# One wide matmul for the high and low rows in the up projection of a gated ConvFFN block

## The chip, the cores and the metric

The kernel runs on one core of a Trainium2 chip. The metric is the device time of one execution in microseconds. The engines are PE (TensorE: matmuls, and PEld for its weight loads), DVE (VectorE), ACT (ScalarE), POOL (GpSimd) and SP (SyncE, which here only issues transfers). Each works through its own queue in order; semaphores between them tell when a result is there.

## The reference

A decoder block with 512 rows and 2048 channels: a recurrent mixer and a windowed attention side by side, then a feed-forward part. All is float32. The change concerns the first product of the feed-forward part:

```python
D_MODEL = 2048
SEQ = 512
D_FF = 5632

def conv_ffn(h, w_up, conv_w, conv_b, w_down):
    u = h @ w_up                                   # (512, 2048) @ (2048, 11264)
    S = u.shape[1]
    up = jnp.pad(u, ((0, 0), (CONV_W - 1, 0), (0, 0)))
    c = up[:, 0:S] * conv_w[0] + up[:, 1:S + 1] * conv_w[1] + up[:, 2:S + 2] * conv_w[2] + conv_b
    val, gate = jnp.split(c, 2, axis=-1)
    return (jax.nn.silu(gate) * val) @ w_down
...
        x = x + conv_ffn(rms_norm(x, norm2_g[l]), w_up[l], conv_w[l], conv_b[l], w_down[l])
```

## The kernel before

The kernel runs in stages: the input projections with mixer and attention, the branch and out products, the **up products** of the feed-forward part with its convolution and gate, and the down products.

*Precision.* A float32 product is made of three faster ones. A weight tile is split into a high part `whi` (rounded by ACT, L1105) and the rest `wlo` (DVE, L1107), and the rows into `xh` and `xl` likewise. The sum is `whi*xh + whi*xl + wlo*xh`: three matmuls, each with its own weight load, into the same PSUM columns (L1122 to L1125).

*Blocks and products.* The up projection works on 44 blocks `f`. A block has 128 value columns and 128 gate columns of the weights; with the two halves of the contraction that is a 2 x 2 of weight tiles (`a11`, `a12`, `a22` and sums), against a 2 x 2 of the rows (two halves of 256 rows, `TH`, and two halves of the contraction, each of `KH` = 8 pieces of 128). A scheme with seven products in place of eight gives the four quarters of the result `u`: P1, P2, P5, P6, P7, Q4 and P3. Each product is 8 x 3 matmuls of 256 columns. The rows' factors lie in SBUF for the whole stage as pairs of tiles `bq[name] = [high, low]` (`b11`, `b21`, `b22`, `t1` to `t4`).

*PSUM.* A block uses three tiles, each a full bank of 512 columns, of which a steady block uses the first 256. X takes P1, P6, P5 and P3 one upon the other and is read after each of them; P7 and Q4 share Y; P2 has Z. A `start` flag is set on the first matmul of P1, P7 and P2.

*What follows a product* (`Block.out`, L1127 to L1156): after P1, P6, P5 and P3 ACT copies X to a quarter of `u` (L1152); after P2, P5 and Q4 DVE adds Z or Y to a quarter (L1154, L1156). `Block.conv` (L1161 to L1185) makes the convolution in five or seven pieces: ACT scales (L1173) and makes the SiLU (L1179), DVE multiplies and adds (L1176, L1181); in odd blocks `factors` (L884 to L888) then forms four factors for the down products, and `Block.keep` (L1187) issues three DMAs for them on ACT's queue (L893 to L895).

*The order* is written out by hand. `steps` lists (block, product); in a steady block it is P7, P6, P2, P5, then P1 of the next block, Q4, P3. `run(i)` first calls `prep(i + 2)`: the weight sum of P6 and P3 (DVE, L1100), one waiting piece of a convolution, `whi` (ACT) and `wlo` (DVE) for the step after next, and the loads that have become possible; then it issues the matmuls of step i, then `out`. There are three buffers for `whi` and `wlo`, and ACT and DVE run at most two products ahead of PE. Every such instruction is wrapped in `pin`, which keeps the written order on its engine.

*Loads.* SP issues 512 KB weight loads (L1091) as buffers come free; POOL adds a second load onto one in flight for the sums s3 and s1 (L1093), and makes sums of down weights on the side (L239).

The blocks 0 to 6 have a special order of their own, and so has block 43.

Of the kernel before, what the change touches and what calls it, by code (L numbers as in the profile page):

```python
# [8 lines left out]
F32 = mybir.dt.float32  # L9
F32R = mybir.dt.float32r  # L10
# [3 lines left out]
ALU = mybir.AluOpType  # L14
# [4 lines left out]
P = 128  # L19
S = 512  # L20
# [114 lines left out]
def block_kernel(ctx: ExitStack, tc: tile.TileContext, d: Dims, a: dict, out: bass.AP):  # L135
    nc = tc.nc
    act, dve, pool, pe, sync = nc.scalar, nc.vector, nc.gpsimd, nc.tensor, nc.sync
    NK, NP, NQ, NKV, NF = d.NK, d.NP, d.NQ, d.NKV, d.NF
# [16 lines left out]
    NPRE = 4  # L155
# [50 lines left out]
    pin = tc.keep_in_program_order  # L206
# [13 lines left out]
    for f in range(NPRE):  # L220
        w, t = a["w_up"][f], {n: up_d[f, n] for n in ("s3", "s1", "P6", "P3")}
# [70 lines left out]
    if True:  # L292
# [3 lines left out]
        with tc.tile_pool(name="x0_ps", bufs=6, space=PSUM) as ps0:  # L296
# [10 lines left out]
            for h in range(2):  # L307
                hs = slice(h * HT * P, (h + 1) * HT * P)
                for k in range(NK):
                    ps = ps0.tile([P, HT * P], F32, name="ps_x", tag="x")  # L310
# [45 lines left out]
        with ExitStack() as pt:  # L356
# [4 lines left out]
            def small():  # L361
                return mps.tile([P, S], F32, name="mi", tag="mi")
# [26 lines left out]
            for t in range(NKV):  # L389
# [12 lines left out]
                ps = small().rearrange("p (n c) -> p n c", c=P)  # L402
                for b in range(NT):
                    pe.transpose(ps[:, b], vf[:, b * P : (b + 1) * P], ident)
                ps = ps.rearrange("p n (h c) -> p n h c", c=HD)
# [14 lines left out]
            for g in range(NHK):  # L420
# [7 lines left out]
                for n in range(NT):  # L428
# [32 lines left out]
                    for kb in kbs:  # L461
                        ps = small().rearrange("p (h c) -> p h c", c=P)
# [3 lines left out]
                    ps = small()  # L466
                    for kb in kbs:
                        for i in range(2):
                            pe.matmul(ps, vhl[:, n - 1 + kb, g].rearrange("p e c -> p (e c)"),
                                      phl[i][:, kb].rearrange("p h c -> p (h c)"),  # L470
                                      start=kb == kbs[0] and i == 0, stop=kb == kbs[-1] and i == 1)
                    ol = ap_.tile([HD, S], F32, name="ol", tag="ol", bufs=2)
                    act.activation(ol, ps[HD:P], AF.Copy)
                    ps, ol = (x[0:HD].rearrange("p (e j c) -> p e j c", e=2, c=P) for x in (ps, ol))
# [6 lines left out]
        with ExitStack() as pr:  # L481
# [8 lines left out]
            for i in range(2):  # L490
                z = zp_.tile([P, S + 1], F32, name=f"zpad{i}")
# [8 lines left out]
            def wtile(tag, bufs=1):  # L500
                return wk.tile([P, S], F32, name=tag, tag=tag, bufs=bufs)
# [20 lines left out]
            for i in range(NG):  # L522
                acc = ztile(d.c_gd + i * P)
                t = wtile("lw")
# [347 lines left out]
    KH = NK // 2  # L872
    TH = S // 2
# [26 lines left out]
    with ExitStack() as pbb:  # L900
# [8 lines left out]
        for m, i in order:  # L909
            hi, lo, r0, n, gi = parts[i]  # L910
# [11 lines left out]
            if second:  # L922
                w = min(XC, d.D)
                for e in range(m * XC, (m + 1) * XC, w):
                    t, c0 = divmod(e, d.D)
# [81 lines left out]

    upx = ExitStack()
    bqp = upx.enter_context(tc.tile_pool(name="bqA", bufs=1, reuse_waits="tile"))
    bq = {n: [bqp.tile([P, KH, TH], F32R, name=f"{n}{i}") for i in range(2)] for n in ("b11", "b21")}  # L1010
    hp = hps.enter_context(tc.tile_pool(name="hhlO", bufs=3, reuse_waits="tile"))
    NCC = d.D // S
    ssp = tcp.tile([P, NT, NCC], F32, name="ssp")
# [62 lines left out]
    us = []  # L1076
    dve.tensor_scalar(cw[:, 0:3, NF:], cw[:, 0:3, NF:], -1.0, None, op0=ALU.mult)

    class Block:

        def __init__(self, f):
            self.f, self.w, self.hl = f, {}, {}
            self.apart = 2 <= f < NPRE

        def load(self, n):
            f, w = self.f, self.w
            at = {"a11": (0, 0), "a12": (0, 1), "s3": (0, 0), "s1": (1, 0), "a22": (1, 1)}
            w[n] = raw_tile("a11", 2) if own(f, n) else raw_tile()  # L1090
            sync.dma_start(w[n], up_d[f, n] if (f, n) in up_d else a["w_up"][(f, *at[n])])  # L1091
            if n in ("s3", "s1") and f >= NPRE:
                pool.dma_start(w[n], a["w_up"][f, 1, int(n == "s1")], accum_op=ALU.add)  # L1093
# [15 lines left out]
        def mm(self, n):  # L1109
            if n == "P1":  # L1110
                x = ups.tile([P, S], F32, name="X", tag="X")
                self.X = x[:, :TH]
                self.Z = x[:, TH:] if self.f < NPRE else upy.tile([P, S], F32, name="Z", tag="Y")[:, :TH]
            if n == "P7":
                self.Y = upy.tile([P, S], F32, name="Y", tag="Y")[:, :TH]
            into = {"P2": "Z", "P7": "Y", "Q4": "Y"}.get(n, "X")
            ps = getattr(self, "Z" if self.apart and n in ("P5", "P3") else into)
            start = n in ("P1", "P7") or n == "P2" and self.f >= NPRE or n == "P5" and self.apart
            whi, wlo = (x.rearrange("p (k c) -> p k c", c=P) for x in self.hl.pop(n))
            xh, xl = bq[{"P1": "b11", "P2": "b21", "P7": "t3", "P6": "t2", "P5": "t1", "Q4": "t4", "P3": "b22"}[n]]  # L1120
            for k in range(KH):
                last = k == KH - 1  # L1122
                for i, (l, r) in enumerate(((whi, xh), (whi, xl), (wlo, xh))):
                    pin(pe.matmul(ps, l[:, k], r[:, k], start=start and k + i == 0, stop=last and i == 2,  # L1124
                                  skip_group_check=True))  # L1125

        def out(self, n):  # L1127
            if n == "P7":
                return
            X, Y, Z = self.X, getattr(self, "Y", None), self.Z  # L1130
            if n == "P1" and self.f < NPRE:
                self.t1 = up.tile([P, TH], F32, name="t1", tag="t1", bufs=NPRE)
                pin(act.activation(self.t1, X, AF.Copy))
                return

            if self.f < NPRE:
                if n == "P2":
                    pin(dve.tensor_tensor(self.t1, self.t1, Z, op=ALU.add))
                    return
                if self.apart and n != "P1":  # L1140
                    if n != "P6":
                        i, j, more = {"P5": (1, 1, (Z, Y)), "P3": (0, 1, (Z,)), "Q4": (1, 0, (Y,))}[n]
                        u = us[self.f % 2][:, i, 2 + j * TH : 2 + (j + 1) * TH]
                        pin(act.activation(u, X, AF.Copy))
                        for ps in more:
                            pin(dve.tensor_tensor(u, u, ps, op=ALU.add))
                    return
            i, j, ps, first = {"P1": (0, 0, X, True), "P2": (0, 0, Z, False), "P6": (1, 0, X, True), "P5": (1, 1, X, True),
                               "Q4": (1, 0, Y, False), "P3": (0, 1, X, True)}[n]
            u = us[self.f % 2][:, i, 2 + j * TH : 2 + (j + 1) * TH]  # L1150
            if first:
                pin(act.activation(u, ps, AF.Copy))  # L1152
                if n == "P5":
                    pin(dve.tensor_tensor(u, u, Y, op=ALU.add))  # L1154
            else:
                pin(dve.tensor_tensor(u, u, ps, op=ALU.add))  # L1156

        def place(self):
            pin(act.activation(us[self.f % 2][:, 0, 2 : 2 + TH], self.t1, AF.Copy))
# [109 lines left out]
    with tc.tile_pool(name="sqp", bufs=1, side="right", reuse_waits="tile") as sqp:  # L1269
# [3 lines left out]
        for i in range(len(PRODUCTS)):  # L1273
            nm = PRODUCTS[i][0]
            last = i == len(PRODUCTS) - 1
# [21 lines left out]


    bqp = upx.enter_context(tc.tile_pool(name="bqB", bufs=1, reuse_waits="tile"))
    bq.update({n: [bqp.tile([P, KH, TH], F32R, name=f"{n}{i}") for i in range(2)] for n in ("b22", "t1", "t3", "t2", "t4")})  # L1300
    up = upx.enter_context(tc.tile_pool(name="upw", bufs=1, side="left", reuse_waits="tile"))

    psx = ExitStack()
# [29 lines left out]
    upy = psx.enter_context(tc.tile_pool(name="uppy", bufs=4, space=PSUM, side="right", reuse_waits="tile"))  # L1333
# [16 lines left out]
    for i in range(2):  # L1350
        u = upu.tile([P, 2, S + 2], F32, name=f"u{i}")
# [36 lines left out]
    with ExitStack() as pd:  # L1388
        pxy = pd.enter_context(tc.tile_pool(name="psD", bufs=1, space=PSUM, reuse_waits="tile"))
        acc = {n: banks(pxy, n) for n in "XY"}  # L1390
        for i in range(len(PRODUCTS)):
            nm = PRODUCTS[i][0]
# [72 lines left out]
def build(nc, arrays, d):  # L1465
    aps = {
        k: nc.dram_tensor(f"in_{k}_dram", v.shape, mybir.dt.from_np(v.dtype), kind="ExternalInput").ap()
        for k, v in arrays.items()
    }
    out = nc.dram_tensor("out_0_dram", (S, d.D), F32, kind="ExternalOutput").ap()  # L1470
    with tile.TileContext(nc) as tc:
        block_kernel(tc, d, aps, out)
# [11 lines left out]
```

## Time and profile before

| | |
|---|---|
| median of 3 runs | 2802.57 us (2802.53 to 2804.05) |
| the profiled execution | 2802.24 us |
| its span in the trace | 2800.5 us |
| mean granted clock of PE | 0.998 |
| stretch of blocks 7 to 42, (7, P7) to (42, P3) | 1632.3 to 2358.1 us |

How to read the rows: the page's first part has an engine's busy time, its share of the span and its number of instructions. A row of the timeline has start, duration (both in us), engine, line of the kernel, operation, `out<-in`, shapes, and in square brackets the idle time of the engine before it and what ended it. A row of sums by stage has the stretch and its length, then for each engine busy time and count. Tile names are those of the program without buffer numbers: `a` is the buffer in which the sums for P6 and P3 are made, `raw` any other weight load, `t` and `b` the rows' factors. An instruction's recorded duration reaches somewhat beyond the point from which the next may start, so pitches are read from start to start.

### The profile page before, as it was taken

Reading aid. Unit: us, or ns where it says so; the run is one execution under the profiler, and the core shown is the slowest. Engines: PE = TensorE matmul, PEld = TensorE weight load, DVE = VectorE, ACT = ScalarE, POOL = GpSimd, SP = SyncE. Lnnn points to the kernel's source line nnn. Section 1 sums busy time; section 2 is a strip of 40 time slices with the busy share of each in tenths; the row PEclk is TensorE's granted clock in tenths of the full one; section 3 lists DMA queues with packets and bytes.
Section 4 is the critical chain, followed back from the end, with each engine's and each line's share of the span. In section 5 each row is a group of like instructions: output and inputs, shape, how many; then the busy total and the mean of one; then the engine's idle time right before and its main releaser. Section 6 shows DMA issues by size and latency. Waiting matters only on the chain.

```text
span 2800.5 us, 45992 instructions
## 1 busy us (share of the span) xinstructions
PE 2759.3 (99%) x17466; PEld 2400.8 (86%) x17466; DVE 1988.9 (71%) x3452; ACT 1352.9 (48%) x2278; POOL 231.3 (8%) x307
## 2 busy tenths in 40 slices
PE   6999999999999999999999999999999999999999
PEld 5777778787778778888889999999999999888887
DVE  5588677877787774545678778787777778655555
ACT  4255445545544553322465555554555555444444
POOL 0001011110111001011000011101010101000000
PEclk9999999999999999999999999999999999999999
DMA  7865887787778767888776888888898888877775
GB/s 221 226 160 161 210 212 187 189 195 192 186 184 198 183 176 216 243 250 283 252 256 186 233 227 227 243 232 222 232 243 229 225 231 237 319 243 240 257 256 187
DMA packets 227182, 619.62 MB, mean 221 GB/s; under 512 B 24832, under 2 KB 44944, under 8 KB 225936
## 3 DMA queue, kind: packets, MB, share of 16 engines
q1 hardware_dynamic: 158400, 441.03, 48.2%
q0 software_dynamic: 37216, 136.33, 25.7%
q10 hardware_dynamic: 31344, 39.31, 4.1%
q8 instruction: 137, 2.24, 0.3%
q14 instruction: 85, 0.70, 0.1%
HBM read 566.96 MB, written 191.18 MB: 271 GB/s over the span
## 4 chain that ended last, share of the span: by engine, by line
PE 63%; DVE 2%; DMA 1%; ACT 1%; issue 0%; ACTq 0%; DVEq 0%; SPq 0%
PE X L1124 17%; PE X L988 10%; PE Y L988 9%; PE Y L1124 9%; PE acc L270 4%; PE acc L269 4%; PE acc L271 4%; PE Z L1124 4%; DMA raw<-in_w_dn_dram 1%; DVE wlo L1107 0%; DVE c L1176 0%; PE psS L761 0%; ACT whi L1105 0%; PE ps_t L1054 0%; PE psG L752 0%
## 5 line engine op out<-in xcount | busy, mean ns | idle before, releaser
L269 PE MATMUL acc<-xhi,whi 128*128 128x512 f32 x1152 | 462.7, 402 | 1.9 <-DVE xlo L315 1.9
L270 PE MATMUL acc<-xlo,whi 128*128 128x512 f32 x1152 | 459.8, 399 | 0.0
L271 PE MATMUL acc<-xhi,wlo 128*128 128x512 f32 x1152 | 459.5, 399 | 0.0
L254 ACT ACTIVATE whi<-raw 128x512 fp32r<-128x512 f32 x352 | 220.5, 630 | 404.9 <-PE acc L270 326.6
L981 DVE TENSOR_TENSOR wlo<-raw,whi 128x1024 fp32r<-128x1024 f32 x210 | 256.7, 1224 | 199.7 <-ACT whi L980 198.2
L980 ACT ACTIVATE whi<-raw 128x1024 fp32r<-128x1024 f32 x210 | 222.5, 1060 | 282.2 <-PE X L988 131.9
L255 DVE TENSOR_TENSOR wlo<-raw,whi 128x512 fp32r<-128x512 f32 x352 | 241.7, 689 | 162.3 <-ACT whi L254 142.7
L1107 DVE TENSOR_TENSOR wlo<-raw,whi 128x1024 fp32r<-128x1024 f32 x184 | 224.6, 1222 | 77.4 <-ACT whi L1105 77.3
L1124 PE MATMUL X<-b,whi 128*128 128x256 f32 x1472 | 268.9, 283 | 0.2 <-ACT whi L1105 0.2
L1124 PE MATMUL X<-t,whi 128*128 128x256 f32 x1408 | 257.2, 283 | 1.4 <-ACT u L1152 1.4
L1124 PE MATMUL Y<-t,whi 128*128 128x256 f32 x1408 | 257.1, 283 | 0.0
L269 PEld LDWEIGHTS acc<-xhi,whi 128*128 128x128 f32 x1152 | 217.0, 188 | 41.7 <-DVE xlo L315 2.1
L271 PEld LDWEIGHTS acc<-xhi,wlo 128*128 128x128 f32 x1152 | 216.8, 188 | 40.0 <-issue 0.9
L270 PEld LDWEIGHTS acc<-xlo,whi 128*128 128x128 f32 x1152 | 217.0, 188 | 39.4 <-issue 1.7
L1124 PEld LDWEIGHTS X<-b,whi 128*128 128x128 f32 x1472 | 229.6, 192 | 0.5 <-ACT whi L1105 0.4
L1105 ACT ACTIVATE whi<-a 128x1024 fp32r<-128x1024 f32 x124 | 130.9, 1056 | 201.3 <-DVE a L1100 195.9
L1124 PEld LDWEIGHTS X<-t,whi 128*128 128x128 f32 x1408 | 219.6, 192 | 1.6 <-ACT u L1152 1.6
L1124 PEld LDWEIGHTS Y<-t,whi 128*128 128x128 f32 x1408 | 219.6, 192 | 0.0
L1124 PE MATMUL X<-b,wlo 128*128 128x256 f32 x736 | 208.5, 283 | 0.9 <-DVE wlo L1107 0.9
L1105 ACT ACTIVATE whi<-raw 128x1024 fp32r<-128x1024 f32 x184 | 192.9, 1049 | 23.0 <-ACT whi L1105 13.9
L1107 DVE TENSOR_TENSOR wlo<-a,whi 128x1024 fp32r<-128x1024 f32 x124 | 151.9, 1225 | 67.6 <-ACT whi L1105 67.0
L1124 PE MATMUL X<-t,wlo 128*128 128x256 f32 x704 | 199.4, 283 | 0.3 <-DVE wlo L1107 0.3
(387 smaller groups left out, 5796.9 us busy)
## 6 DMA issues: line engine op xcount, KB each, us to landing
raw<-in_w_up_dram SPq DMA_DIRECT2D x170, 512.0 KB
raw<-in_w_z_dram SPq DMA_DIRECT2D x288, 256.0 KB
s_dn<-in_w_dn_dram POOLq DMA_DIRECT2D x88, 512.0 KB, 7.4
raw<-s_dn SPq DMA_DIRECT2D x88, 512.0 KB
raw<-in_w_up_dram POOLq DMA_DIRECT2D x80, 512.0 KB, 8.5
raw<-in_w_dn_dram SPq DMA_DIRECT2D x66, 512.0 KB
s_dn<-in_w_dn_dram SPq DMA_DIRECT2D x44, 512.0 KB
s_dn<-s_dn SPq DMA_DIRECT2D x44, 512.0 KB
```

The lines of the kernel that those rows point to most:

```text
L254: act.activation(hi, raw, AF.Copy)
L255: dve.tensor_tensor(lo, raw, hi.bitcast(F32), op=ALU.subtract)
L269: stream.append(pe.matmul(acc, whi[:, j], xhi[:, k], start=first, stop=False))
L270: stream.append(pe.matmul(acc, whi[:, j], xlo[:, k], start=False, stop=False))
L271: stream.append(pe.matmul(acc, wlo[:, j], xhi[:, k], start=False, stop=last))
L980: act.activation(whi, wr, AF.Copy)
L981: dve.tensor_tensor(wlo, wr, whi.bitcast(F32), op=ALU.subtract)
L988: pe.matmul(dst, l[:, q, ts], r[:, es], start=fst and j == 0, stop=lst and j == 2, skip_group_check=True)
L1105: pin(act.activation(hi, t, AF.Copy))
L1107: return lambda: pin(dve.tensor_tensor(lo, t, hi.bitcast(F32), op=ALU.subtract))
L1124: pin(pe.matmul(ps, l[:, k], r[:, k], start=start and k + i == 0, stop=last and i == 2, skip_group_check=True))
```

## The change

In blocks 7 to 42 five of the seven products (P7, Q4, P2, P5, P3) pass `xh` and `xl` in one matmul: `whi` is the weight of a matmul with 512 moving columns, the first 256 from the high tile and the others from the low one, into the full bank. `wlo*xh` stays a matmul of 256 columns into the first half. So each of the 8 pieces of such a product takes two matmuls and two weight loads instead of three. The high and low tiles of a factor become halves of one tile (`bqt`). The second half of the bank then has to be added as well: `out` adds the second half of Z after P2, those of Y and X after P5, that of Y after Q4 and that of X after P3, each as one more DVE instruction on the same quarter of `u`. P1 and P6 stay as they were; P5 and P3 add into the bank X of the running sum.

```diff
-    bq = {n: [bqp.tile([P, KH, TH], F32R, name=f"{n}{i}") for i in range(2)] for n in ("b11", "b21")}
+    bqt = {n: bqp.tile([P, 2, KH, TH], F32R, name=n) for n in ("b11", "b21")}
+    bq = {n: [t[:, i] for i in range(2)] for n, t in bqt.items()}
...
+    WIDE = ("P7", "Q4", "P2", "P5", "P3")
...
-            self.f, self.w, self.hl = f, {}, {}
+            self.f, self.w, self.hl, self.full = f, {}, {}, {}
             self.apart = 2 <= f < NPRE
+            self.wide = WIDE if NPRE + 3 <= f < NF - 1 else ()
...
                 self.X = x[:, :TH]
-                self.Z = x[:, TH:] if self.f < NPRE else upy.tile([P, S], F32, name="Z", tag="Y")[:, :TH]
+                z = x if self.f < NPRE else upy.tile([P, S], F32, name="Z", tag="Y")
+                self.Z = x[:, TH:] if self.f < NPRE else z[:, :TH]
+                self.full.update(X=x.rearrange("p (e s) -> p e s", e=2), Z=z.rearrange("p (e s) -> p e s", e=2))
             if n == "P7":
-                self.Y = upy.tile([P, S], F32, name="Y", tag="Y")[:, :TH]
+                y = upy.tile([P, S], F32, name="Y", tag="Y")
+                self.Y = y[:, :TH]
+                self.full["Y"] = y.rearrange("p (e s) -> p e s", e=2)
...
             for k in range(KH):
                 last = k == KH - 1
+                if n in self.wide:
+                    pin(pe.matmul(self.full[into], whi[:, k], bqt[nm][:, :, k], start=start and k == 0, stop=False,
+                                  skip_group_check=True))
+                    pin(pe.matmul(ps, wlo[:, k], xh[:, k], start=False, stop=last, skip_group_check=True))
+                    continue
                 for i, (l, r) in enumerate(((whi, xh), (whi, xl), (wlo, xh))):
                     pin(pe.matmul(ps, l[:, k], r[:, k], start=start and k + i == 0, stop=last and i == 2,
                                   skip_group_check=True))
...
+            adds = [Y] if n == "P5" else []
+            adds += [self.full["Y"][:, 1]] if n in ("P5", "Q4") and "P7" in self.wide else []
+            adds += [self.full["Z"][:, 1]] if n == "P2" and n in self.wide else []
+            adds += [self.full["X"][:, 1]] if n in ("P5", "P3") and n in self.wide else []
             if first:
                 pin(act.activation(u, ps, AF.Copy))
-                if n == "P5":
-                    pin(dve.tensor_tensor(u, u, Y, op=ALU.add))
             else:
-                pin(dve.tensor_tensor(u, u, ps, op=ALU.add))
+                adds.insert(0, ps)
+            for more in adds:
+                pin(dve.tensor_tensor(u, u, more, op=ALU.add))
```

The factors that are made later (`b22`, `t1` to `t4`) are allocated in the same way, as one tile each.

More of the change, by code (lines that the diff above doesn't have):

```diff
@@ L1119, in mm @@
             whi, wlo = (x.rearrange("p (k c) -> p k c", c=P) for x in self.hl.pop(n))
-            xh, xl = bq[{"P1": "b11", "P2": "b21", "P7": "t3", "P6": "t2", "P5": "t1", "Q4": "t4", "P3": "b22"}[n]]
+            nm = {"P1": "b11", "P2": "b21", "P7": "t3", "P6": "t2", "P5": "t1", "Q4": "t4", "P3": "b22"}[n]
+            xh, xl = bq[nm]
             for k in range(KH):
                 last = k == KH - 1
+                if n in self.wide:
[3 more added lines that the diff above has]
+                    continue
                 for i, (l, r) in enumerate(((whi, xh), (whi, xl), (wlo, xh))):
@@ L1299, in block_kernel @@
     bqp = upx.enter_context(tc.tile_pool(name="bqB", bufs=1, reuse_waits="tile"))
-    bq.update({n: [bqp.tile([P, KH, TH], F32R, name=f"{n}{i}") for i in range(2)] for n in ("b22", "t1", "t3", "t2", "t4")})
+    bqt.update({n: bqp.tile([P, 2, KH, TH], F32R, name=n) for n in ("b22", "t1", "t3", "t2", "t4")})
+    bq.update({n: [t[:, i] for i in range(2)] for n, t in bqt.items()})
     up = upx.enter_context(tc.tile_pool(name="upw", bufs=1, side="left", reuse_waits="tile"))
```

## The prediction

> **What bounds the kernel now.** First the page, for which engine is full; then the sums by stage, for the stage that the change touches.
>
> ```profile
> PE 2759.3 (99%) x17466; PEld 2400.8 (86%) x17466; DVE 1988.9 (71%) x3452; ACT 1352.9 (48%) x2278; POOL 231.3 (8%) x307
> 1632.33:2358.09 725.76, 725.76 (x6051) 725.76 (x6049) 571.97 (x686) 372.21 (x505) 76.96 (x90) 1.00 0.86 233
> 2500.00:2620.00 120.00, 120.00 (x531) 99.34 (x531) 71.90 (x75) 58.39 (x67) 0.00 (x0) 1.00 0.75 242
> ```
>
> The second row runs from the first matmul of (7, P7) to (42, P3): the 36 blocks whose `wide` is not empty. Its columns are the stretch, PE, PEld, DVE, ACT and POOL busy, granted clock, DMA share and GB/s. PE has no gap in it. Three of its 6051 matmuls only overlap the edges, so 36 x 7 x 8 x 3 = 6048 matmuls of 256 columns take 725.76 us: 120.0 ns each, 20.16 us a block, 40.32 us for two. The third row lies in the down products, also without a gap: some 529 matmuls of 512 columns in 120.00 us, 226.7 ns each. So a column costs (226.7 - 120.0) / 256 = 0.417 ns and a matmul 13.3 ns besides. DVE is 79% busy in the stage; that leaves the question of who holds the next place, and a share of busy time can't answer it.
>
> The timeline can. DVE and ACT work their queues in written order, and hand work to each other: ACT makes `whi`, DVE then `wlo`; DVE sums the weights for P6 and P3 (L1100), ACT then rounds that sum. I followed one lap of this, from DVE's sum for P6 to the same sum a block later. First DVE, then ACT, for the lap of an odd block:
>
> ```profile
> 1912.57 1.22 DVE L1100 TENSOR_TENSOR a<-a,raw 128x1024 f32<-128x1024 f32 x1
> 1913.70 0.41 DVE L887 SCALAR_TENSOR_TENSOR tq<-tq,c 128x256 f32<-128x256 f32 x1
> 1914.15 0.42 DVE L888 SCALAR_TENSOR_TENSOR tq<-tq,c 128x256 f32<-128x256 f32 x1
> ...
> 1918.22 1.23 DVE L1107 TENSOR_TENSOR wlo<-raw,whi 128x1024 fp32r<-128x1024 f32 x1 [0.20 <-ACT whi L1105]
> 1919.36 0.75 DVE L1176 SCALAR_TENSOR_TENSOR c<-u,par,c 128x512 f32<-128x512 f32 x1
> ...
> 1923.67 1.23 DVE L1107 TENSOR_TENSOR wlo<-a,whi 128x1024 fp32r<-128x1024 f32 x1
> 1924.81 0.42 DVE L1156 TENSOR_TENSOR u<-u,Z 128x256 f32<-128x256 f32 x1
> 1925.14 0.74 DVE L1176 SCALAR_TENSOR_TENSOR c<-u,par,c 128x512 f32<-128x512 f32 x1
> 1925.81 1.22 DVE L1107 TENSOR_TENSOR wlo<-raw,whi 128x1024 fp32r<-128x1024 f32 x1
> 1926.94 0.41 DVE L1154 TENSOR_TENSOR u<-u,Y 128x256 f32<-128x256 f32 x1
> 1927.27 1.22 DVE L1100 TENSOR_TENSOR a<-a,raw 128x1024 f32<-128x1024 f32 x1
> ...
> 1932.05 0.42 DVE L1156 TENSOR_TENSOR u<-u,Y 128x256 f32<-128x256 f32 x1
> 1932.39 1.22 DVE L1100 TENSOR_TENSOR a<-a,raw 128x1024 f32<-128x1024 f32 x1
> ```
>
> ```profile
> 1913.90 1.06 ACT L1105 ACTIVATE whi<-a 128x1024 fp32r<-128x1024 f32 x1 [3.42 <-DVE a L1100]
> ...
> 1916.42 0.82 ACT L1173 ACTIVATE c<-u,par 128x512 f32<-128x512 f32 x1 [1.19 <-DVE wlo L1107]
> 1917.14 1.04 ACT L1105 ACTIVATE whi<-raw 128x1024 fp32r<-128x1024 f32 x1
> 1920.14 0.63 ACT L1179 ACTIVATE c<-c 128x512 f32<-128x512 f32 x1 [1.95 <-DVE c L1176]
> 1920.68 1.04 ACT L1105 ACTIVATE whi<-raw 128x1024 fp32r<-128x1024 f32 x1
> 1921.62 0.36 ACT L1152 ACTIVATE u<-X 128x256 f32<-128x256 f32 x1
> 1921.89 0.80 ACT L1173 ACTIVATE c<-u,par 128x512 f32<-128x512 f32 x1
> 1922.59 1.05 ACT L1105 ACTIVATE whi<-a 128x1024 fp32r<-128x1024 f32 x1
> ...
> 1926.29 0.38 ACT L1152 ACTIVATE u<-X 128x256 f32<-128x256 f32 x1 [1.70 <-PE X L1124]
> ```
>
> Read in one order of time: sum for P6 (1912.57), `whi` of it (1913.90), the copy of P3 and three DMA issues of `keep` on ACT's queue, convolution (1916.42), `whi` (1917.14), `wlo` (1918.22), convolution (1919.36), SiLU (1920.14), `whi` for P5 (1920.68), copy (1921.62), convolution (1921.89), `whi` (1922.59), `wlo` (1923.67), add of Z (1924.81), convolution (1925.14), `wlo` (1925.81), add of Y (1926.94), sum for P3 (1927.27), and by `whi` and `wlo` for P3 and P7 to the add of Y (1932.05) and the sum (1932.39). Each starts when the one before allows. One row names PE: ACT's copy of P5 waits for it (1926.29), but is done at 1926.67, before DVE reaches the add of Y that needs it. This lap of 19.82 us is a closed chain of DVE and ACT, 0.34 us shorter than PE's block.
>
> The lap before it, of an even block, does wait for PE:
>
> ```profile
> 1892.07 1.22 DVE L1100 TENSOR_TENSOR a<-a,raw 128x1024 f32<-128x1024 f32 x1
> ...
> 1904.57 1.22 DVE L1107 TENSOR_TENSOR wlo<-raw,whi 128x1024 fp32r<-128x1024 f32 x1
> 1906.55 0.42 DVE L1154 TENSOR_TENSOR u<-u,Y 128x256 f32<-128x256 f32 x1 [0.76 <-ACT u L1152]
> ```
>
> ```profile
> 1893.40 1.06 ACT L1105 ACTIVATE whi<-a 128x1024 fp32r<-128x1024 f32 x1 [3.04 <-DVE a L1100]
> 1894.61 0.39 ACT L1152 ACTIVATE u<-X 128x256 f32<-128x256 f32 x1
> ...
> 1899.14 1.04 ACT L1105 ACTIVATE whi<-raw 128x1024 fp32r<-128x1024 f32 x1
> 1900.37 0.38 ACT L1152 ACTIVATE u<-X 128x256 f32<-128x256 f32 x1 [0.19 <-PE X L1124]
> ```
>
> A copy follows a `whi` 0.94 us after its start where it need not wait (1920.68, 1921.62), an add follows a `wlo` after 1.13 (1925.81, 1926.94). Here it is 1.21, 1.23 and 1.98: waits of 0.27, 0.29 and 0.85 us, together 1.41. The lap takes 20.50, both 40.32: PE's pace. **DVE and ACT alone would need 40.32 - 1.41 = 38.9 us for two blocks. That 1.4 us is all they have to give.**
>
> **The change, part by part.** *Matmuls.* In 36 x 5 x 8 = 1440 places two matmuls of 256 columns become one of 512: PE loses 1440 x 13.3 ns = 19.2 us, a pair of blocks 1.07 us, to 39.25. The trace before has no moving operand in two pieces 8 KB apart; if reading it is slower, 80 such matmuls a pair would have to lose over 40 ns each to use up the 3.4 us that PE, as shown below, will idle. At nothing gained or lost I cost it.
>
> *Adds.* `out` now adds the second half of each bank: one more DVE instruction for P2, two for P5, one for Q4, one for P3, all of 128x256 from PSUM into the same `u`. An add that is followed by other work costs 0.33 us of the queue (1924.81 to 1925.14). But successive adds here update one `u`, each reading what the last wrote. The row for that is the pair L887, L888, where the second reads the first's `t2`: 1913.70 to 1914.15, 0.45 us. That is SBUF alone; with a PSUM operand the price lies between 0.33 and, by the nearest row, 0.45, and I take 0.45. So P2 goes from 0.33 to 0.45 + 0.33, P5 from 0.33 to 0.45 + 0.45 + 0.33, Q4 from 0.33 to 0.45 + 0.33: 0.45 + 0.90 + 0.45 = 1.80 us a block, each on the lap above (Z, Y and Y there). P3's new add stands behind `wlo` for P6, ahead of the convolution. In laps with `keep` ACT's DMA issues cover it: DVE is free from 1913.90 + 1.08 + 1.14 = 1916.12, and the convolution on ACT ends at 1917.24. In the others, counted without the waits for PE, DVE is free at 1893.40 + 1.08 + 1.14 = 1895.62; the add (0.33) and the convolution (0.67) end at 1896.62, while ACT's convolution could start at 1893.40 + 0.94 + 0.27 = 1894.61 and `wlo` for P2 at 1894.61 + 0.72 + 1.08 = 1896.41: 0.2 us late. (0.27 is from copy to convolution, as at 1921.62; 0.72 from that to `whi`, 1.08 on to `wlo`, 1.14 on to DVE's next, as from 1916.42 to 1919.36.) The pair: 2 x 1.80 + 0.2 = 3.8.
>
> The Trainium skill speaks against my 0.45: its page "VectorE: DVE Perf Modes", section "The DRAIN you can't avoid", says that eight copies take the same time with a semaphore after each as with one at the end. By that rule the pair would give 2 x 1.34 + 0.2 = 2.9; the 0.45 beside the 0.33 in this trace disagrees with it.
>
> *New waits.* Q4's first matmul waits for the second read of Y, P3's for that of X. Q4 starts one product (2.88 us) after P5 ends, and copy and two adds take some 1.3 us; behind Q4 all of PE would queue. I cost them at nothing as long as DVE is under 1.5 us late there; later, `wlo` for P3 is late by more. *Tiles.* High and low rows in one tile, and full banks where halves were named: the tiles were 512 wide already, no bytes are added, no DMA, nothing on SP's or POOL's queue. Nothing.
>
> *Sum.* Two blocks of DVE and ACT: 38.9 + 3.8 = 42.7 us, against PE's 39.25. The chain passes PE and becomes the bound: PE now idles 3.4 us a pair before `wlo` and `whi`, first of all at P3, and before P6, P2 and P5 of odd blocks, behind `keep`. Against today's 40.32 that is +2.4 us a pair, times 18 pairs 43 us; the 1.4 us in hand at the entry, and a little at block 43, are used up once: **+41 us**. The profiled execution took 2802.24 us (span 2800.5 and 1.7 around it), 0.33 under the median of the runs shown; with it the forecast is 2843.5 us.
>
> **Rivals.** *PE stays the bound, faster.* If DVE and ACT keep up, only the 19.2 us count: 2783. For it: DVE is at 79%, and 180 adds of 0.33 to 0.45 us bring it to about 90% of a shorter stage. Against: the lap of 19.82 us without a wait for PE, which utilization hides. It decides where the pair stays below 39.25, so where the adds cost under 0.4 us a pair in place of 3.8. The page "TensorE: Matmul & The Clock Gate" of the Trainium skill, section "Wait — 56ns, not 53.3ns?", puts the fixed cost of a matmul at 2.5 ns; by that this rival would gain only 3.6 us, but the two pitches above give 13.3.
>
> *Short adds.* All at 0.33: 38.9 + 2.9 = 41.8, +1.5 a pair, 27 less 2: 2827.
>
> *A wait of ACT on the whole `u`.* If the first piece of the convolution, which reads the gate's half of `u`, also waits for P3's new add into the value half, then ACT, with the next `whi` and SiLU behind it, waits in even laps until 1895.62 + 0.42 = 1896.04 instead of 1894.61: 1.4 us, of which 0.2 is counted. In odd laps `keep` covers nearly all. Some 0.2 added for those makes +1.4 a pair: 2868. Against it: the two halves are separate addresses.
>
> *The wide matmul is not wide* (it runs as two). Then PE's pair stays 40.32, still below 42.7: 2843 as well; only the pitch would tell.
>
> **How the numbers follow.** Forecast 0.62 (with the last rival in it), PE-bound 0.12, short adds 0.14, whole `u` 0.10, and 0.02 for no difference. A measurement of this kernel can tell about 0.2% (5.6 us) from no change. Faster is the second alone, 0.12; same 0.02; slower 0.86. The range takes in the short adds and the whole `u`: 2820 to 2870.
>
> **What would show it.** PE: 346.7 ns for each pair of a wide and a narrow matmul within a product. PE's idle time in the stage goes from none to some 60 us, on L1124's first matmuls with `wlo`, released by DVE's `wlo`. The two laps sum to 42.7, with no row of DVE or ACT that waits for PE; second adds start 0.45 us after first ones. Before 1632 and after the stage nothing changes. I am wrong if PE still shows no gap, if the second add starts after 0.33, or if ACT's convolution waits for DVE's add of P3.

## The result and the profile after

The changed kernel takes 2833.83 us (median of 4 runs, 2830.49 to 2837.37) against 2802.63 us of the kernel before on the same chip (4 runs): a ratio of 1.011, interval 1.0097 to 1.0122. It is slower by 31 us; the forecast was 41 slower.

First the page of the changed kernel: each engine's share, and the chain that ended last. The last row is that chain in the kernel before.

```profile
PE 2767.2 (98%) x16026; PEld 2326.7 (82%) x16026; DVE 2052.7 (72%) x3632; ACT 1346.9 (48%) x2278; POOL 231.8 (8%) x307
PE 44%; DVE 12%; ACT 6%; issue 3%; DMA 2%; ACTq 0%; DVEq 0%; SPq 0%
```

```profile
PE 63%; DVE 2%; DMA 1%; ACT 1%; issue 0%; ACTq 0%; DVEq 0%; SPq 0%
```

TensorE has 1440 matmuls fewer, and VectorE its 180 adds more (3632 against 3452), 64 us more of busy time. The chain that ended last has moved: VectorE and ScalarE now hold 18% of the span and not 3%. The stage shows it in its sums (columns as in the prediction), and in what TensorE waits for (engine and line, what ended the wait, us in total, times, longest):

```profile
1636.05:2391.00 754.95, 730.60 (x4613) 649.33 (x4611) 634.47 (x864) 366.84 (x506) 76.79 (x89) 1.00 0.83 224
```

```profile
PE X L1135 <- DVE wlo L1111: 19.6, 35, 0.6
PE X L1138 <- DVE wlo L1111: 4.7, 19, 0.5
```

The 36 blocks take 754.95 us and not 725.76. TensorE, before without a gap, waits for `wlo` at P3 (L1135) and at P6 (L1138). The idle time (24 us) is less than what the waits cost: a stall is measured from the modelled end of the matmul before. At P3 of the trace's block below, 1925.14 to 1926.05 is 0.91 us where a wide matmul is otherwise followed after 0.23, yet the row says 0.51.

```profile
1925.14 0.40 PE L1133 MATMUL X<-b,whi 128*128 128x512 f32 x1
1926.05 0.38 PE L1135 MATMUL X<-b,wlo 128*128 128x256 f32 x1 [0.51 <-DVE wlo L1111]
1926.27 0.40 PE L1133 MATMUL X<-b,whi 128*128 128x512 f32 x1
1926.50 0.28 PE L1135 MATMUL X<-b,wlo 128*128 128x256 f32 x1
1926.62 0.40 PE L1133 MATMUL X<-b,whi 128*128 128x512 f32 x1
...
1928.62 0.28 PE L1135 MATMUL X<-b,wlo 128*128 128x256 f32 x1
1928.74 0.40 PE L1133 MATMUL Y<-t,whi 128*128 128x512 f32 x1
```

The same lap as in the prediction, on VectorE (the timeline's rows of after; "x2" is two adds in one row):

```profile
1907.26 1.22 DVE L1104 TENSOR_TENSOR a<-a,raw 128x1024 f32<-128x1024 f32 x1
...
1910.83 0.41 DVE L1174 TENSOR_TENSOR u<-u,X 128x256 f32<-128x256 f32 x1
...
1918.41 0.87 DVE L1174 TENSOR_TENSOR u<-u,Z 128x256 f32<-128x256 f32 x2
...
1920.99 0.87 DVE L1174 TENSOR_TENSOR u<-u,Y 128x256 f32<-128x256 f32 x2
1921.97 0.42 DVE L1174 TENSOR_TENSOR u<-u,X 128x256 f32<-128x256 f32 x1
1922.36 1.23 DVE L1104 TENSOR_TENSOR a<-a,raw 128x1024 f32<-128x1024 f32 x1
...
1927.72 0.87 DVE L1174 TENSOR_TENSOR u<-u,Y 128x256 f32<-128x256 f32 x2
1928.50 1.22 DVE L1104 TENSOR_TENSOR a<-a,raw 128x1024 f32<-128x1024 f32 x1
...
1932.07 0.41 DVE L1174 TENSOR_TENSOR u<-u,X 128x256 f32<-128x256 f32 x1
...
1949.36 1.22 DVE L1104 TENSOR_TENSOR a<-a,raw 128x1024 f32<-128x1024 f32 x1
```

The sums for P6 are the marks of the laps: 1907.26, 1928.50, 1949.36, so 21.24 and 20.86 us where there were 20.50 and 19.82. From the first such sum of the stage to the last (36 laps, rows of before and then of after):

```profile
1630.73 1.22 DVE L1100 TENSOR_TENSOR a<-a,raw 128x1024 f32<-128x1024 f32 x1
2353.95 1.22 DVE L1100 TENSOR_TENSOR a<-a,raw 128x1024 f32<-128x1024 f32 x1
```

```profile
1634.52 1.22 DVE L1104 TENSOR_TENSOR a<-a,raw 128x1024 f32<-128x1024 f32 x1
2387.29 1.22 DVE L1104 TENSOR_TENSOR a<-a,raw 128x1024 f32<-128x1024 f32 x1
```

The stage takes 723.22 us before and 752.77 after, 29.6 more; a pair of blocks 40.32 and 41.9 (median of the pairs). The two profiled executions differ by 33.4 us (2835.61 and 2802.24). The other 3.8 us are there at the stage's entry already, and 3.7 of them at the first matmul of the up products (1474.62 before, 1478.30 after), ahead of every matmul and add that the change touches. In the profiled executions of this study that first matmul comes between 1473.7 and 1481.0 us, and the entry, with what the experiments change in blocks 0 to 6, between 1624 and 1638. So I compare kernels below by the stage, from first sum to last, and take the whole time beside it.

### The profile page after: what moved, and what is told of

Read it like the earlier page. It is cut to its first block, busy times and chain, and to the rows that moved or that the text cites. A ratio compares the mean times of both kernels' runs of the same rounds, so it can differ in the third digit from the quotient of the medians.

```text
span 2833.5 us, 43431 instructions
## 1 busy us (share of the span) xinstructions
PE 2767.2 (98%) x16026; PEld 2326.7 (82%) x16026; DVE 2052.7 (72%) x3632; ACT 1346.9 (48%) x2278; POOL 231.8 (8%) x307
## 4 chain that ended last, share of the span: by engine, by line
PE 44%; DVE 12%; ACT 6%; issue 3%; DMA 2%; ACTq 0%; DVEq 0%; SPq 0%
PE X L988 11%; PE Y L988 9%; DVE wlo L1111 5%; PE X L1138 5%; ACT whi L1109 4%; PE acc L270 4%; PE acc L269 4%; PE acc L271 4%; DVE a L1104 2%; DVE u L1174 2%; DVE c L1194 2%; PE Y L1138 1%; PE Y L1133 1%; PE X L1133 1%; ACT c L1191 1%
## 5 line engine op out<-in xcount | busy, mean ns | idle before, releaser
L1133 PE MATMUL Y<-t,whi 128*128 128x512 f32 x576 | 206.3, 398 | 0.0
L988 PE MATMUL X<-whi,hhi 128*128 128x512 f32 x480 | 187.1, 390 | 1.2 <-ACT u L1170 1.2
L988 PE MATMUL X<-whi,hlo 128*128 128x512 f32 x480 | 186.9, 389 | 0.0
L988 PE MATMUL X<-wlo,hhi 128*128 128x512 f32 x480 | 186.9, 389 | 0.0
L1138 PE MATMUL X<-b,whi 128*128 128x256 f32 x896 | 163.8, 283 | 0.2 <-ACT whi L1109 0.2
L1135 PE MATMUL Y<-t,wlo 128*128 128x256 f32 x576 | 161.7, 281 | 0.0
L1138 PE MATMUL X<-t,whi 128*128 128x256 f32 x832 | 152.5, 283 | 1.4 <-ACT u L1170 1.4
L239 POOL DMA_DIRECT2D s_dn<-in_w_dn_dram x88 | 73.0, 829 | 884.7 <-DMA s_dn<-in_w_dn_dram 371.8
```

The lines of the kernel that those rows point to most:

```text
L988: pe.matmul(dst, l[:, q, ts], r[:, es], start=fst and j == 0, stop=lst and j == 2, skip_group_check=True)
L1133: pin(pe.matmul(self.full[into], whi[:, k], bqt[nm][:, :, k], start=start and k == 0, stop=False, skip_group_check=True))
```

## The experiments

**The loop theory**, the prediction's: VectorE and ScalarE form a closed chain from block to block; the added adds lengthen it past TensorE. **Rival A**: the wide matmuls themselves are slow, or their new waits for banks. **Rival B**: the adds cost as a sum of VectorE's work, whatever reads what.

In the table the time is the median of a kernel's runs, and the ratio is to the kernel before as it ran beside it (medians of 2802.6 to 2804.5 us). Pair and stage come from the profiled execution. A pair is two blocks, here as the median over the stage.

| kernel | time, us | ratio to before (interval) | pair, us | stage, us |
|---|---|---|---|---|
| before | 2802.6 | 1 | 40.32 | 723.2 |
| after | 2833.8 | 1.011 (1.0097 to 1.0122) | 41.9 | 752.8 |
| e1, no adds | 2794.4 | 0.9965 (0.9952 to 0.9978) | 39.8 | 713.2 |
| e2, adds alone | 2833.5 | 1.0107 (1.0093 to 1.0121) | 41.8 | 751.5 |
| e3, adds apart | 2811.7 | 1.0029 (1.0017 to 1.0040) | 40.8 | 732.6 |
| e4, after, SiLU later | 2797.5 | 0.9978 (0.9969 to 0.9986) | 40.1 | 722.9 |
| e5, before, SiLU later | 2798.4 | 0.9980 (0.9971 to 0.9989) | 40.32 | 723.7 |
| e6, `keep` on GpSimd | 2834.9 | 1.0110 (1.0096 to 1.0124) | 42.0 | 752.9 |
| e7, P2 and P3 wide | 2802.0 | 0.9990 (0.9981 to 0.9999) | 40.1 | 719.0 |
| f1, e4 side by side | 2797.2 | 0.9978 (0.9969 to 0.9987) | 40.1 | 722.8 |
| f2, e4 wide first | 2791.9 | 0.9959 (0.9946 to 0.9971) | 40.0 | 719.2 |
| g1, after, `wlo` last | 2833.6 | 1.0106 (1.0092 to 1.0120) | 42.0 | 753.4 |
| g2, g1 with SiLU later | 2782.6 | 0.9926 (0.9914 to 0.9939) | 39.45 | 709.3 |
| h1, before with both | 2796.6 | 0.9974 (0.9964 to 0.9984) | 40.32 | 723.7 |

### e1, the wide matmuls without their adds

```diff
-            adds += [self.full["Y"][:, 1]] if n in ("P5", "Q4") and "P7" in self.wide else []
-            adds += [self.full["Z"][:, 1]] if n == "P2" and n in self.wide else []
-            adds += [self.full["X"][:, 1]] if n in ("P5", "P3") and n in self.wide else []
```

> The wide matmuls alone: the second halves of the banks (the part high weights times low rows of the five products) are left out of the sum, all else as in the changed kernel. Loop theory (DVE and ACT hand work to each other in a closed lap, and the adds lengthen it): two blocks of DVE and ACT need some 38.1 us again, PE 39.25, so PE bounds and the kernel gains the 19.2 us of the merged matmuls: 2783 us. Rival A (the wide matmul itself or PE's new waits for the reads of X and Y cost the time): the matmuls are still there, so at least 2815 us. Rival B (DVE has too much to do in all): 2783 us too.

The 38.1 us in the expectation are the loop of before as worked out from the result, 41.9 - 3.8; the prediction had 38.9. The run took 2794.4 us: faster than before, so the matmuls are not what made the change slow, but 11 us above what was expected. TensorE has no gap in the stage, and the 39.8 us of a pair are its own:

```profile
1640.00:2340.00 700.00, 700.00 (x4510) 634.49 (x4509) 555.81 (x668) 364.65 (x495) 75.95 (x88) 1.00 0.86 237
```

So a wide and a narrow matmul cost more than 346.7 ns. The rows of P3 above show it in after: from 1926.27 to 1928.74 go seven pieces, 353 ns each. Over e1's stage, from start to start, the narrow one comes 236 ns after the wide one (mean; 224 to 242) and the next wide one 117 after the narrow: 353 against 3 x 120.0 = 360. A merged place saves 7 ns and not 13.3: 0.56 us a pair, 10 us in all and not 19.2.

### e2, the adds without the wide matmuls

The three matmuls a piece are narrow again; the five adds stay and read the first halves of the banks.

```diff
-                if n in self.wide:
+                if False:
...
-            adds += [self.full["Z"][:, 1]] if n == "P2" and n in self.wide else []
+            adds += [self.full["Z"][:, 0]] if n == "P2" and n in self.wide else []
```

(and so for Y and X)

> The adds alone: three narrow matmuls as before the change, and the same five adds more a block, which read the first halves of the banks a second time (so those halves are counted twice in u). Loop theory: two blocks of DVE and ACT need 41.9 us as in the changed kernel, PE 40.32, so the lap bounds: 2831 us. Rival A: no wide matmul, no cost, 2803 us. Rival B: 2831 us.

2833.5 us, the time of after: the adds alone cost all of it. Rival A, that the loss lies in the wide matmul or its waits, has fallen.

### e3, the same adds, but none reads what the last one wrote

Every follow-up add goes to a tile of its own (fp16, 128x256) instead of `u`.

```diff
-            for more in adds:
-                pin(dve.tensor_tensor(u, u, more, op=ALU.add))
+            for j, more in enumerate(adds):
+                if j == 0:
+                    pin(dve.tensor_tensor(u, u, more, op=ALU.add))
+                else:
+                    pin(dve.tensor_tensor(apart[j], bq["b11"][0][:, 0].bitcast(F32), more, op=ALU.add))
```

> As the changed kernel, with as many adds, but each second or third add of a product reads a row factor in place of u and writes a small buffer (float16) in place of u, so none waits for the one before it; the second halves of Z, Y (and of X after P5) thereby are left out of u. Loop theory with the 0.45 us pitch of dependent adds: each of the four follow-ups a block starts 0.11 us sooner, 0.9 us a pair, 41.0 us in place of 41.9: 2815 us. Rival B (the number of DVE instructions counts, not their order) and rival A: no change, 2831 us.

2811.7 us, 3 below what was expected; the same number of adds, of the same 0.41 us each, cost 22 us less than in after. VectorE's timeline of e3:

```profile
1911.29 0.41 DVE L1175 TENSOR_TENSOR u<-u,Y 128x256 f32<-128x256 f32 x1
1911.62 0.41 DVE L1177 TENSOR_TENSOR ap<-b,Y 128x256 f16<-128x256 f32 x1
1911.95 0.41 DVE L1177 TENSOR_TENSOR ap<-b,X 128x256 f16<-128x256 f32 x1
1912.28 1.22 DVE L1104 TENSOR_TENSOR a<-a,raw 128x1024 f32<-128x1024 f32 x1
```

An independent add starts 0.33 us after the one before. In after, two adds that update one `u` take 0.87 from the first's start to the second's end (1920.99), of which the second is 0.42: it starts 0.45 later. The add of X after P5 starts later still: 1921.97 is 0.53 after the second add of Y (1921.97 less 1921.44), and 0.52 to 0.53 in all 36 blocks; in e2, where it reads the first half of X, it is 0.45. Why the second half costs the 0.07 more stays open. A pair has 8 follow-up adds on the loop: 6 x 0.12 + 2 x 0.19 = 1.1 us, and by 1.1 the pairs differ. Rival B, which knows no difference between the two kernels, has fallen.

### e4 and e5, a link of the loop taken out

The odd lap runs through SiLU on ScalarE, which stands ahead of `whi` and waits 2 us for VectorE's convolution. Both kernels let it run two parts later: e4 is after with that edit, e5 before with it.

```diff
-                if part == 1:
-                    pin(act.activation(t, t, AF.Silu))
+                if part == 3:
+                    pin(act.activation(self.c[1], self.c[1], AF.Silu))
```

> The changed kernel in full, with ACT's SiLU moved from the second piece of a convolution to the fourth, so that the next products' high weights no longer stand behind it on ACT; the amount of work of each engine is the same. Loop theory: the lap loses the step from DVE's second piece to ACT's SiLU and back, 1.9 us or more of some 20.9, two blocks then need under 38.2 us, PE's 39.25 bounds and the gain of the matmuls comes through: 2784 us (2780 to 2792). Rival A and rival B: no change, 2831 us.

> A control for e4: the kernel before with SiLU in conv part 3 and nothing else. Loop theory: before is bound by TensorE in this stage (240 matmul pitches of 120 ns make 40.3 us a pair whatever the loop does), so the shorter loop brings nothing: 2803, at most 2 us less. If the SiLU's place was a cost of its own, whatever the change: 2796 to 2798 as in e4, and e4 would show nothing of the change.

In e5's expectation 240 pitches should be 336 (2 x 7 x 8 x 3); 336 x 120.0 ns are the 40.32 us. e4 took 2797.5 us, 36 less than after: with the loop shortened, all that the adds cost is gone. But it missed 2784 by 13, and e5 shows that the little it wins over before isn't the change's: e5 is as fast. e5's 5 us don't lie in the steady stage (40.32 a pair in both) but ahead of it: from the first matmul of the up products to the stage's entry are 156.1 us in before and 150.6 in e5. Most of it is in blocks 4 to 6, where TensorE has gaps in before. The stretch from 1560 to 1640 us, before and then e5:

```profile
1560.00:1640.00 80.00, 76.14 (x621) 74.71 (x620) 64.45 (x84) 40.67 (x59) 7.75 (x9) 1.00 0.80 215
```

```profile
1560.00:1640.00 80.00, 79.87 (x664) 79.51 (x663) 67.87 (x90) 44.15 (x61) 8.61 (x10) 1.00 0.87 242
```

3.9 us of idle time become 0.1. So the SiLU's place cost the kernel before some 5 us too; my expectation for e5 (2803) was wrong in that, right for the stage. In e4 the change itself gains nothing in the stage: 722.9 against e5's 723.7. TensorE's pair falls by only 0.2 us, since 0.56 is all that the wide matmuls save, some 0.35 go to stalls, mostly for `wlo` at P6, and the first lap of the stage is 1.3 us longer than e5's (21.43 and 20.16; why, I did not find).

### f1 and f2, what the wide matmul costs

f1 is e4 with the high and low 256 columns of one piece side by side in the tile; f2 is e4 with the eight wide matmuls of a product ahead of its eight narrow ones.

```diff
-    bqt = {n: bqp.tile([P, 2, KH, TH], F32R, name=n) for n in ("b11", "b21")}
-    bq = {n: [t[:, i] for i in range(2)] for n, t in bqt.items()}
+    bqt = {n: bqp.tile([P, KH, 2, TH], F32R, name=n) for n in ("b11", "b21")}
+    bq = {n: [t[:, :, i] for i in range(2)] for n, t in bqt.items()}
...
-                    pin(pe.matmul(self.full[into], whi[:, k], bqt[nm][:, :, k], start=start and k == 0, stop=False,
+                    pin(pe.matmul(self.full[into], whi[:, k], bqt[nm][:, k], start=start and k == 0, stop=False,
```

> The kernel after with SiLU in conv part 3 (as e4, 2797 us), and with the high and low part of one k stored side by side, so that the wide matmul's 512 columns are one run and not two of 256 that lie 8 KB apart. In e4 and e1 a wide matmul is followed by its narrow one after 236 ns and the narrow by the next wide after 117 (353 a k), where the prediction had 226.7 + 120. If the two runs cost the missing ns: 236 falls to 227, some 80 x 6.7 to 9 ns = 0.5 to 0.7 us a pair, 10 to 12 us in all, 2785 to 2788. If it is the mixture of 512 and 256 columns (a weight load that the pitch can't hide): 236 stays and the time is 2797.

> As e4, but in a product with wide matmuls its eight wide ones come first and its eight narrow ones after them. If the missing ns come from the change of width (a wide one beside narrow neighbours): wide to wide is 227 ns, narrow to narrow 120, and the time 2785 to 2788. If they belong to the wide matmul itself (its two runs, or a cost per column that is higher than taken): wide to wide stays at 233 to 236 or more, the product costs 353 to 356 ns a k as before, and the time is 2797 (up to 2802).

f1 took 2797.2 us, with the same 236 and 117 ns: the two pieces 8 KB apart cost nothing. f2 took 2791.9, between its two expected times. Its timeline of TensorE, a product in two rows:

```profile
1903.36 2.00 PE L1133 MATMUL X<-b,whi 128*128 128x512 f32 x8
1905.20 1.11 PE L1141 MATMUL X<-b,wlo 128*128 128x256 f32 x8
1906.15 0.40 PE L1133 MATMUL Y<-t,whi 128*128 128x512 f32 x1
```

Eight wide matmuls in 1.84 us are 230 ns each, eight narrow ones in 0.95 some 119: 349 to 350 a piece against 353. So about half of the missing 6.3 ns (353 against 346.7) come from the alternation of widths. A wide one is still followed by a wide one after 230.6 ns (mean over the stage) against 226.7 in the down products; that rest stays open.

### e6, the stores of `keep`

```diff
-            store_factors(act, "dn", self.f // 2, B[self.f - 1].c[0], self.c[0], self.tq, pin)
+            store_factors(pool, "dn", self.f // 2, B[self.f - 1].c[0], self.c[0], self.tq, pin)
```

> The kernel after with the three stores of c's factors issued by GpSimd's queue and not by ScalarE's; SiLU where it was. Corrected loop theory: in the kernel before these three issues, held up behind a copy of X that waited for TensorE, made 0.84 us of the slack that the prediction missed; in the kernel after they already run beside the whi copy, and only the third (1931.11 to 1931.52, some 0.4 us) still stands in the odd lap's loop. So at most 0.4 us a pair is won: 2826 to 2834. The prediction's own view (slack 1.41, the issues outside of the sum): 2834. If the issues cost ScalarE their full 1.2 us in each odd lap: 2812.

2834.9 us: nothing won, and just above the expected 2826 to 2834. ScalarE's convolution now starts 1.23 us after the `whi` that it followed after 1.68 in after; the odd laps become 20.6, but the even ones 21.2 and, every other time, 21.5, with a wait in front of an add of X (VectorE, e6) that after doesn't have:

```profile
1923.62 0.42 DVE L1174 TENSOR_TENSOR u<-u,X 128x256 f32<-128x256 f32 x1 [0.47 <-DVE u L1174]
```

What that add waits for, its row doesn't tell. It is settled that the issues are not worth 1.2 us a lap in after.

### e7, adds that fit into what is in hand

```diff
-    WIDE = ("P7", "Q4", "P2", "P5", "P3")
+    WIDE = ("P2", "P3")
```

> The kernel after with only P2 and P3 wide, and so only their two adds of a second half; SiLU where it was. Loop theory: P2's add costs 0.45 a block and P3's 0.2 a pair, 1.1 us a pair against the some 2.25 us that VectorE and ScalarE have in hand: TensorE stays the bound, without a wait for wlo, at 40.32 less 32 x 7 ns = 40.1 us a pair, 2799 to 2800. If each add costs its share of what five cost, whatever is in hand: 2 of 5 of the 28 us that e2 lost in the stage, 2812 to 2815.

The pair takes 40.1 us, as the loop theory had it, the stage 719.0 against 723.2, and TensorE has no wait for `wlo` in it. The whole time, 2802.0, is 2 us above the expected 2799 to 2800; this profiled execution entered the stage 6.8 us later than that of before. Two of the five adds cost nothing where all five cost 28 us (e2's stage): there is a threshold, not a price for each add.

### g1 and g2, `wlo` at the end of each product

If TensorE's stalls ahead of `wlo` were a part of the loop, needing `wlo` later would shorten it.

```diff
             for k in range(KH):
-                last = k == KH - 1
                 if n in self.wide:
                     pin(pe.matmul(self.full[into], whi[:, k], bqt[nm][:, :, k], start=start and k == 0, stop=False,
                                   skip_group_check=True))
-                    pin(pe.matmul(ps, wlo[:, k], xh[:, k], start=False, stop=last, skip_group_check=True))
                     continue
-                for i, (l, r) in enumerate(((whi, xh), (whi, xl), (wlo, xh))):
-                    pin(pe.matmul(ps, l[:, k], r[:, k], start=start and k + i == 0, stop=last and i == 2,
-                                  skip_group_check=True))
+                for i, r in enumerate((xh, xl)):
+                    pin(pe.matmul(ps, whi[:, k], r[:, k], start=start and k + i == 0, stop=False, skip_group_check=True))
+            for k in range(KH):
+                pin(pe.matmul(ps, wlo[:, k], xh[:, k], start=False, stop=k == KH - 1, skip_group_check=True))
```

> The kernel after with the matmuls with wlo at the end of each product, in all blocks, SiLU where it was. TensorE then needs wlo some 1.9 us later, and its stalls at P3 and P6 ahead of wlo have no place left. Loop theory (the pair of 41.9 us is a chain of VectorE and ScalarE alone, TensorE's wait is its effect): the pair stays at 41.7 to 41.9, TensorE's idle time moves to the first matmul of some product, which then waits for whi, and the time is 2830 to 2836. Rival (the stall at P3 is a part of the loop, since a later product is late by it and the copy of its bank with it): the pair falls by 0.7 to 1.3 us, 2810 to 2822.

> As g1 with SiLU in conv part 3 (f2 with wlo last in P1 and P6 too). f2 left TensorE one wait a pair, some 0.5 us for wlo at P6. If VectorE and ScalarE then keep below TensorE: 40.32 less 80 x 10.4 ns = 39.5 us a pair, 18 x 0.48 = 9 us below f2: 2783. If their loop without TensorE is at f2's 39.97 already: 2792, with the idle time ahead of whi. Rival of the wide matmul's price (no gain from fewer instructions): 2798, as the kernel before with the same place of SiLU.

g1 took 2833.6 us, as after. Not one wait for `wlo` is left, and the time has not moved. TensorE's waits in g1:

```profile
PE Y L1132 <- DVE u L1173: 14.4, 33, 0.4
PE X L1136 <- ACT whi L1109: 4.9, 17, 0.3
PE X L1132 <- ACT u L1169: 0.8, 4, 0.3
```

It waits elsewhere now, for VectorE's adds to free Y and for `whi`. A wait that can be removed without any effect on the time was an effect itself: the loop of VectorE and ScalarE sets the pace. g2, with that loop shortened by SiLU's place, took 2782.6 (expected 2783). Its stage:

```profile
1640.00:2340.00 700.00, 700.00 (x4545) 640.60 (x4544) 624.69 (x850) 359.42 (x497) 76.76 (x89) 1.00 0.87 237
```

TensorE without a gap, VectorE 89% busy (624.69 of 700) and yet not in its way. The pair of 39.45 us is TensorE's own: 40.32 less 80 x 10.4 ns.

### h1, the control: both edits without the change

h1 is e5 with the matmuls with `wlo` at each product's end.

> The kernel before with both side edits of g2 (SiLU in conv part 3, the matmuls with wlo at the end of each product) and nothing of the change: a control for g2's 2782.6 us. Loop theory: the steady stage stays at TensorE's 40.32 us a pair, since three matmuls of 120 ns a k are left, and the time is that of e5, 2796 to 2799; the change itself is then worth some 14 to 15 us beside these edits. If g2's gain came from the order of the matmuls: 2783 to 2788.

2796.6 us and 40.32 a pair. So beside these two edits the change is worth 14 us (2796.6 to 2782.6), and alone it costs 31. g2 is faster than both kernels of the case, by 22 us against before; 8 of these are the two edits' own.

## Why the prediction was right, and where its sizes were off

**The mechanism was right.** That the loop of VectorE and ScalarE would pass TensorE and become the bound is shown three ways: the adds alone cost all (e2), TensorE's stalls can be removed without effect (g1), and a link less in the loop gives the loss back (e4). The 41 us forecast and the 29.6 measured in the stage are the same sum with one term mis-sized, the time in hand. A second term, the matmuls' gain, was too large as well but had no part in the result.

**The time in hand: 1.41 us a pair was too little.** 38.9 + 3.8 should have given 42.7; the pair takes 41.9. With the adds at 3.9 (3.8, and 2 x 0.07 for X) the loop before needs 41.9 - 3.9 = 38.0, which is 2.3 us in hand; e3, with 8 follow-up adds of 0.33 and the same 0.2, says 40.8 - 2.84 = 37.9, or 2.4. I had counted the waits that are visible as a late `whi`, copy or add. One more hid in the odd lap, where I had taken `keep` for a fixed cost of the queue. ScalarE's queue in before, then TensorE's end of P3 there, then ScalarE in after:

```profile
1914.78 0.34 ACTq L893 DMA_DIRECT2D h_dn<-c  x1
1914.86 0.37 ACT L1152 ACTIVATE u<-X 128x256 f32<-128x256 f32 x1
1915.15 0.47 ACTq L894 DMA_DIRECT2D h_dn<-c  x1
1916.00 0.37 ACTq L895 DMA_DIRECT2D h_dn<-tq  x1
```

```profile
1914.45 0.28 PE L1124 MATMUL X<-b,wlo 128*128 128x256 f32 x1
1914.57 0.40 PE L1124 MATMUL Y<-t,whi 128*128 128x256 f32 x2
```

```profile
1929.84 1.06 ACT L1109 ACTIVATE whi<-a 128x1024 fp32r<-128x1024 f32 x1 [3.89 <-DVE a L1104]
1929.88 0.34 ACTq L893 DMA_DIRECT2D h_dn<-c  x1
1930.26 0.47 ACTq L894 DMA_DIRECT2D h_dn<-c  x1
1930.80 0.37 ACT L1170 ACTIVATE u<-X 128x256 f32<-128x256 f32 x1
1931.11 0.37 ACTq L895 DMA_DIRECT2D h_dn<-tq  x1
1931.52 0.81 ACT L1191 ACTIVATE c<-u,par 128x512 f32<-128x512 f32 x1 [0.35 <-issue]
```

In before, `whi` ran from 1913.90, but the first DMA issue came at 1914.78, just after P3's last matmul ended (1914.45 + 0.28 = 1914.73). The copy of P3 ahead of it in the queue waited for TensorE; ScalarE was busy with `whi` meanwhile, so no idle time shows. From `whi` to convolution were 2.52 us (1913.90, 1916.42). In after, P3 is done at 1928.90, before `whi` starts, the issues run beside `whi`, and it is 1.68: 0.84 us less. 1.41 + 0.84 = 2.25, against the 2.3 and 2.4 of the two sums. The other odd laps show the same: from `whi` to convolution it is 2.37 us in before, 2.27 in e1 and 2.36 in e7, where TensorE is the bound, and 1.52 in after, 1.53 in e2 and 1.55 in e3, where the loop is (medians). With SiLU moved it is short although TensorE is the bound (1.61 in e4, 1.56 in g2), so there the wait falls elsewhere. That the hidden wait is this one is read from the rows and agrees in size; no run isolates it. The error is worth 0.84 x 18 = 15 us, of which the longer first lap of the stage (21.34 after 19.69) and the 2 us that I had taken off at entry and end give back a part.

**The adds: right but for the 0.07 of X.** It is 0.45 us for an add that reads what the last wrote and 0.33 for an independent one. The short-adds rival came near in the total (2827) by chance, since it took the same 1.41 us in hand. e3 refutes its step: only independent adds start after 0.33. The page "VectorE: DVE Perf Modes" of the Trainium skill, section "The DRAIN you can't avoid", measured no cost of a semaphore after each of eight copies. If that held for the adds here, e3 and after would take the same; they differ by 22 us.

**The matmuls: 13.3 ns a merged place was too much**, 7 are measured and 10.4 with the wide ones in a row. It changed nothing in the result, since TensorE wasn't the bound; it is most of why my expectations for e1 and e4 were too low by 11 and 13 us. I had taken the cost of a column from a product where all matmuls are 512 wide.

**TensorE's waits:** at P3 and P6 ahead of `wlo`, as said, not before P2 and P5; 24 us of recorded idle time and not 60. 18 x (41.9 - 39.8) = 38 is what the pairs leave, and the modelled ends of matmuls hide some 0.2 to 0.3 of each of the 54 stalls. One sign was not as forecast: in all 36 blocks ScalarE's copy of P5 still waits for TensorE, 49 us in sum. It is off the loop, though: the copy ends some 1 us before VectorE's add of Y needs it (1920.02 and 1920.99 in the lap above).

**The whole-`u` rival** had no part: ScalarE's convolution starts before VectorE's added X of P3, at 1931.52 and 1932.07 in the odd lap and at 1909.82 and 1910.83 in the even one, so it doesn't wait for it. **The PE-bound rival**: once its condition held, in g2, TensorE was the bound. That g2's 2782.6 is also that rival's 2783 is chance: 14 of g2's 22 us are the change, not 19.2, and the others are the two edits' own.

## What to carry to other kernels

Before you give work to an engine that is 80% busy, follow one whole lap of its dependences to the same instruction a block later and count the waits for the bound engine in it; that, and not the idle share, is what there is to spend: 2.3 us a pair here, while VectorE could be 89% busy without harm once a link was gone (g2). Look for such waits also where the waiting engine is busy: a queue's DMA issue that comes late shows one that no idle time does. And a stall of the bound engine is a cause only if the time falls when the stall is removed.

## What the runs showed of the hardware

Two adds on one tile start 0.45 us apart, and independent ones 0.33 (128x256, after and e3). A matmul of 512 columns is followed by its like after 226.7 ns in the down products and 230.6 in runs of eight (f2). Where it alternates with one of 256 (e1, f1) that one comes after 236, and the next wide one 117 after that and not 120; two pieces of moving operand 8 KB apart cost nothing (f1).
